# A trunk kernel's first mixer: modulation steps moved behind the gating, weight splits moved to VectorE, two engines put in written order

## The chip, the cores and the metric

The kernel runs on one core of a Trainium2 chip. The metric is the device time of one execution in microseconds (us); smaller is better. The engines are named as in the profile: PE (TensorE, matrix products), PEld (its weight loads), DVE (VectorE), ACT (ScalarE), POOL (GpSimd) and SP (SyncE, which here only issues DMA transfers). Each engine runs its own list of instructions in a fixed order and waits at the head of that list.

## The reference, cut to what matters

Two trunk layers, each a mixer and a gated feed-forward block, for 128 context tokens and 512 latent tokens. The change is all in the mixer of layer 0:

```python
sh1, sc1, g1, sh2, sc2, g2 = split(silu(c) @ w_mod[0] + b_mod[0], 6)   # for each of two streams
h = x * (1 + sc1) + sh1
z = h @ w_in
u = gelu(z[..., :512]);  v = gelu(z[..., 512:1024]);  p = z[..., 1024:]
vn = (v - mean(v)) * rsqrt(var(v) + eps)
s = einsum('hpq,bnqhc->bnphc', w_s, vn) + b_s         # spatial gate, chunks of 128 tokens
y_a = u * s
y_b = (pool_windows_2_4_8_16(p) - p) @ w_pool * pool_scale
x = layernorm(ALPHA * x + g1 * (concat(y_a, y_b) @ w_out))
```

`sh2`, `sc2` and `g1` (with `g2`, from later loads) are the modulation vectors not needed for `h`, but for what follows the mixer's output product.

## The kernel before, in words

All matrix products of this part are made in three passes of reduced-precision numbers: each operand is split into a high part (a cast) and a low part (operand minus high part), and line 152 multiplies high by high, line 153 high by low, line 154 low by high. A weight of 128x1024 is loaded into one of 4 buffers (tiles `r`), cast by ACT at line 99, and subtracted at line 102 by POOL or DVE into a pair of the 12 buffers `w`. `want` lists the weights in order with the engine for the subtraction, `load` starts a transfer, `prep` does the split, `take` hands out the next pair.

The first part (`even_first`) goes over eight slices e of the model width. For each slice `mod(e)` forms the slice's shift and scale on PE from 1 MB of weights (L717), ACT copies the result out (L720), `turn(e)` transposes it on PE (L726) and makes `h` on ACT and DVE (L728 to L737), and `product(e, 0..3)` adds the slice into four results in PSUM (L749 to L751): two output blocks of `u` and two token blocks of `v`. `warm` puts transposes of a unit matrix on PE. In the kernel before only PE's order is the written one in this part (`manual_schedule`); ACT, DVE and POOL are ordered by the scheduler, which builds each engine's list from priorities.

The second part (`even_mixer`) computes the three other token blocks of `v`, normalizes them (L812, L813, L158, L159 for the statistics, L818 for the scaling), and the `u` blocks 2 and 3, each of which is a pass of 48 products on PE into one of two PSUM tiles `A`. Then come four gatings (L871 on PE, five token blocks each; L874, L875, L878 on DVE) and four pooling passes p0 to p3. A pooling pass is again 48 products; ACT copies it out (L887, L888), DVE sums windows (L897 to L908), and `pool_out` multiplies by `w_pool` (six products). After that `out_proj` multiplies by `w_eo`.

Beside this runs the modulation that is needed later, as generators in the list `back`. Each `tick()` advances the first generator by one step. The first of them (`mod_vec`, L241 to L252) computes `sh2` on DVE: eight steps, each with two multiply-and-sum instructions of 128x1024 (L247). The second (`mod_pe`) computes `g1` and `sc2` on PE: eight steps, each with two 512 KB transfers (L281) and two bursts of small products (L292); after the last of them ACT copies the sums out (L298), PE transposes them (L302), DVE copies and adds (L306, L252), and `rows_out` transposes the result (L215) and writes it to memory (L217, L219), first for `g1`, then for `sc2`. `drain()` runs what is left of the generators, and `out_proj` follows.

Of the kernel before, what the change touches and what calls it, by code (L numbers as in the profile page):

```python
# [19 lines left out]
D = 1024  # L20
# [21 lines left out]
def tile_hybrid_trunk(ctx, tc, xT, x, vecs, tabs, wm0, wm1, wmT, crow, grow, lnrow, bs, w_u, w_v, w_p, w_s, w_pool, w_eo,  # L42
# [4 lines left out]
    dve, act, pe, pool, sp = nc.vector, nc.scalar, nc.tensor, nc.gpsimd, nc.sync  # L47
# [19 lines left out]
    def S(shape, dt=F32):  # L67
        return spool.tile(shape, dt, tag="s", name=nm("s"))

    def W(shape, dt=F32):  # L70
        return wpool.tile(shape, dt, tag="w", name=nm("w"))
# [22 lines left out]
    def f(ap):  # L94
        return ap.bitcast(F32)
# [16 lines left out]
    def want(src, shape, scale=None, lo=None):  # L112
        queue.append((src, shape, scale, lo))

    def load():
        src, shape, scale, lo = queue.pop(0)
        raw = R(shape)
        sp.dma_start(raw, src)
        loaded.append((raw, shape, scale, lo))

    def prep(lo_eng=None, pin=False):
        if not loaded:
            load()
        raw, shape, scale, lo_ = loaded.pop(0)
        lo_eng = lo_eng or lo_
        if scale is not None:
            dve.tensor_scalar(raw, raw, scale, ATTN_SCALE, ALU.mult, ALU.mult)
        hi, lo = W(shape, F32R), W(shape, F32R)
        with tc.high_priority() if urgent[0] else ExitStack():
            i = split(hi, lo, raw, act, lo_eng or pool)  # L130
        if pin:
            tc.keep_in_program_order(i)
        ready.append((hi, lo))
# [9 lines left out]
    def take():  # L143
        if not ready:
            prep()
        u = ready.pop(0)
        return u
# [17 lines left out]
    def tick(n=1):  # L165
        for _ in range(n):
            while back:
                try:
                    next(back[0])
                    break  # L170
                except StopIteration:
                    back.pop(0)
# [500 lines left out]
    def even_first(cb):  # L673
        want(w_u[0], [128, D])
        want(w_u[1], [128, D])
        want(w_v[0], [128, 2, 512])
        for k in range(1, 4):
            want(w_v[k], [128, 2, 512])
        for n in range(2, 4):
            want(w_u[n], [128, D], None, dve if n == 2 else None)  # L680
        for n in range(4):
            want(w_p[n], [128, D], None, dve if n % 2 == 0 else None)
        for k in range(8):
            want(w_eo[k], [128, D], None, dve if k >= 4 else None)

        xs = []
        wj = []

        def load_w(e):
            ts_ = [S([128, 4, 256]) for _ in range(2)]  # L690
            for q in range(2):
                sp.dma_start(ts_[q], wm0[e, q])
            wj.append(ts_)

        def load_x(e):
            t = Y([128, T])
            sp.dma_start(t, xT[e])
            xs.append(t)

        load_w(0)  # L700
        load_x(0)
        sp.dma_start(vec, vecs)
        load(), load(), load()
        b0 = cpool.tile([128, 8, 2], F32, name="b0")
        dve.tensor_copy(b0, vec[:, V_B0:V_B0 + 16].rearrange("p (e b) -> p e b", b=2))
        dve.tensor_scalar(b0[:, :, 1], b0[:, :, 1], 1.0, None, ALU.add)
        m0 = cpool.tile([128, 8, 2, 2], F32, name="m0")
        h = new_h()
        pad_h(h)
        psu = [A(), A()]  # L710
        psv = [B(), B()]

        def mod(e):
            ps = B()
            for k in range(8):
                g = k % 4
                pe.matmul(ps[32 * g:32 * g + 32, :256], sc32[:, k, :], wj[e][k // 4][:, k % 4, :],  # L717
                          start=k < 4, stop=k >= 4, tile_position=(0, 32 * g))
            r = Tm([128, 256])
            act.copy(r, ps[:, :256])  # L720
            return r

        def turn(e, r):
            pt = B()
            for b in range(2):
                pe.transpose(pt[:, b * 128:(b + 1) * 128], r[:, b * 128:(b + 1) * 128], ident)  # L726
            p4 = pt[:, :256].rearrange("p (b g s) -> p s b g", b=2, s=32)
            dve.tensor_reduce(m0[:, e], p4[:, 0:2], AX.X, ALU.add)  # L728
            dve.tensor_tensor(m0[:, e], m0[:, e], b0[:, e:e + 1, :].to_broadcast([128, 2, 2]), ALU.add)
            hi, lo = hk(h, e, slice(0, T))  # L730
            t = Tm([128, T])
            for s, (a, b) in enumerate(((0, 128), (LAT0, T))):
                sh, sc = m0[:, e, s, 0:1], m0[:, e, s, 1:2]
                act.activation(hi[:, a:b], xs[e][:, a:b], AF.Identity, bias=sh, scale=sc)
                dve.tensor_scalar(t[:, a:b], xs[e][:, a:b], sc, sh, ALU.mult, ALU.add)
            for (a, b) in ((0, 128), (LAT0, T)):
                dve.tensor_tensor(lo[:, a:b], t[:, a:b], f(hi[:, a:b]), ALU.subtract)  # L737

        def product(k, n):
            if n < 2:  # L740
                w = (us[n][0][:, k * 128:(k + 1) * 128], us[n][1][:, k * 128:(k + 1) * 128])
                for (s, m, c) in G:
                    part(psu[n][:, c:c + m], w, hk(h, k, slice(s, s + m)), k)
            else:
                w = (vu[k // 2][0][:, k % 2, :], vu[k // 2][1][:, k % 2, :])
                part(psv[n - 2], hk(h, k, slice(TOK[n - 2], TOK[n - 2] + 128)), w, k)

        def part(out, a, b, k):
            pe.matmul(out, a[0], b[0], start=k == 0, stop=False)  # L749
            pe.matmul(out, a[0], b[1], start=False, stop=False)  # L750
            pe.matmul(out, a[1], b[0], start=False, stop=k == 7)  # L751

        for e in range(1, 5):
            load_w(e)
            load_x(e)
            if e % 2 == 0:
                load()

        def warm(n):
            for _ in range(n):  # L760
                pe.transpose(psv[0][:, 0:128], ident, ident)

        vu, us = [], []
        with tc.manual_schedule(engines={mybir.EngineType.PE}):
            warm(16)
            r = mod(0)
            warm(3)
            turn(0, r)
            for e in (dve, pool, dve):
                prep(e)  # L770
            us.extend([take(), take()])
            vu.append(take())
            warm(8)
            r = mod(1)
            for e in range(8):
                product(e, 0)
                if e < 7:
                    turn(e + 1, r)
                product(e, 1)
                product(e, 2)  # L780
                if e < 6:
                    r = mod(e + 2)
                    if e + 5 < 8:
                        load_w(e + 5)
                        load_x(e + 5)
                        if e == 1:
                            load()
                product(e, 3)
                if e in (0, 2, 4):
                    prep()  # L790
                    vu.append(take())
        sp.dma_start(tab, tabs)
        for s in range(2):
            sp.dma_start(cb[s], crow[s:s + 1].to_broadcast([128, D]))
        load()
        return h, vu, psu, psv

    def even_mixer(make_norm, nxt_sub):
        cb = [V([128, D]) for _ in range(2)]
        h, vu, psu, psv = even_first(cb)  # L800
# [31 lines left out]
        for i in range(2, 5):  # L832
            c = slice(TOK[i], TOK[i] + 128)
            ps = B()
            mm3(ps, [(*hk(h, k, c), vu[k // 2][0][:, k % 2, :], vu[k // 2][1][:, k % 2, :]) for k in range(8)])
            v_scale(i - 2)
            if i == 2:
                bsb = S([128, 4, 128])
                sp.dma_start(bsb, bs.to_broadcast([128, 512]))
                wst = S([128, 4, 128])  # L840
                sp.dma_start(wst, w_s)
                wp_raw = R([128, 4, 128])
                sp.dma_start(wp_raw, w_pool)
            tick(2)
            v_stats(i, ps)
        v_scale(3)
        for n in range(2, 4):
            u = take()
            hold[0] = 3
            pump()  # L850
            ps = A()
            ntile(u, h, ps)
            u_out(n, ps)
            if n == 2:
                v_scale(4)
            else:
                wp = (W([128, 4, 128], F32R), W([128, 4, 128], F32R))
                split(wp[0], wp[1], wp_raw, act, pool)
            tick(2)
        back.append(mod_pe(0, (2, 4)))  # L860
        tick()
        ycat = ([None] * 4, [None] * 4)
# [689 lines left out]
```

## Time and profile before

| | |
|---|---|
| median of 3 runs | 1537.13 us (1536.52 to 1538.94) |
| the profiled execution | 1539.92 us |
| its span | 1538.10 us |
| PE busy | 1470.3 us, 96% |
| PEld busy | 1324.0 us, 86% |
| DVE busy | 993.5 us, 65% |
| ACT busy | 597.4 us, 39% |
| POOL busy | 569.8 us, 37% |
| PE in the chain that ended last | 31% of the span |

The span is cut into 40 slices on the page; the first four, some 154 us, hold all that the change touches. PE is busy 7, 9, 8 and 9 tenths there, against 9 in nearly all the others. The mean granted clock of PE over the execution is 0.977 of full speed.

### The profile page before, as it was taken

The page shows a single profiled execution, that of the slowest core. Times are in us where ns is not written, and L with a number is a line of the kernel's source. Part 1 is how long each engine was busy: PE and PEld are TensorE (multiplying, and loading weights), DVE is VectorE, ACT ScalarE, POOL GpSimd, SP SyncE. Part 2 cuts the span into 40 slices and gives each one's busy share as a digit, 9 for nine tenths or more (in the row PEclk, how much of TensorE's full clock was granted, in tenths as well). Part 3 has the DMA queues.
Part 4 walks back from the last instruction along what each step waited for, and adds up shares of the span by engine and source line. Part 5 has one row for each costly group of instructions (what it writes and reads, how often), then busy time and mean ns, then how long its engine had stood idle before and what let it go on. Part 6 is the DMA issues. An engine that isn't in the chain of part 4 may idle for free. (4 is left out here: it accounts for less than half of the span.)

```text
span 1538.1 us, 21978 instructions
## 1 busy us (share of the span) xinstructions
PE 1470.3 (96%) x8768; PEld 1324.0 (86%) x8768; DVE 993.5 (65%) x1491; ACT 597.4 (39%) x889; POOL 569.8 (37%) x445
## 2 busy tenths in 40 slices
PE   7989999999999999999979999998999999999997
PEld 5866879989898989888968788787998989898995
DVE  4775687547867797677789577767854424333557
ACT  3422354333141323235755566526433323232323
POOL 2231444333242524543476301764423232142343
PEclk9989999999999999999989899999999999999998
DMA  9544706235443544333011002351533313133231
GB/s 377 215 163 155 273 33 199 97 124 178 153 167 130 168 164 155 113 144 108 26 65 52 7 1 86 121 191 35 199 101 119 114 61 96 34 110 110 69 110 69
DMA packets 54757, 188.10 MB, mean 122 GB/s; under 512 B 6592, under 2 KB 7168, under 8 KB 54656
## 3 DMA queue, kind: packets, MB, share of 16 engines
q1 hardware_dynamic: 54656, 186.71, 35.8%
q8 instruction: 69, 1.13, 0.3%
q14 instruction: 32, 0.26, 0.1%
HBM read 175.96 MB, written 10.72 MB: 121 GB/s over the span
## 5 line engine op out<-in xcount | busy, mean ns | idle before, releaser
L102 POOL TENSOR_TENSOR w<-r,w 128x1024 fp32r<-128x1024 f32 (+3 forms) x136 | 339.9, 2509 | 681.6 <-ACT w L99 681.3
L152 PE MATMUL A<-s,w 128*128 128x258 f32 (+1 forms) x1672 | 525.6, 315 | 11.7 <-DVE t L556 4.5
L153 PE MATMUL A<-s,w 128*128 128x258 f32 (+1 forms) x1672 | 523.3, 313 | 0.5 <-DVE s L102 0.5
L154 PE MATMUL A<-s,w 128*128 128x258 f32 (+1 forms) x1672 | 522.3, 313 | 1.1 <-POOL w L102 1.1
L152 PEld LDWEIGHTS A<-s,w 128*128 128x128 f32 x1672 | 319.1, 191 | 23.0 <-issue 13.3
L153 PEld LDWEIGHTS A<-s,w 128*128 128x128 f32 x1672 | 319.4, 191 | 4.2 <-issue 2.5
L154 PEld LDWEIGHTS A<-s,w 128*128 128x128 f32 x1672 | 319.6, 191 | 3.9 <-issue 2.5
L99 ACT CAST w<-r 128x1024 fp32r<-128x1024 f32 (+3 forms) x184 | 186.1, 1029 | 343.4 <-PE B L153 137.4
L153 PE MATMUL B<-w,s 128*128 128x512 f32 (+2 forms) x734 | 284.2, 387 | 6.0 <-DVE w L102 6.0
L152 PE MATMUL B<-w,s 128*128 128x512 f32 (+2 forms) x734 | 284.5, 389 | 4.1 <-DVE y L492 2.9
L154 PE MATMUL B<-w,s 128*128 128x512 f32 (+2 forms) x734 | 283.1, 387 | 1.0 <-DVE s L102 1.0
L555 DVE SCALAR_TENSOR_TENSOR t<-A,vec,t 128x641 f32<-128x641 f32 x88 | 77.7, 883 | 218.5 <-ACT t L554 218.5
L153 PEld LDWEIGHTS B<-w,s 128*128 128x128 f32 x734 | 139.9, 191 | 33.8 <-DVE w L102 7.1
L152 PEld LDWEIGHTS B<-w,s 128*128 128x128 f32 x734 | 140.1, 191 | 32.3 <-DVE y L492 3.5
L154 PEld LDWEIGHTS B<-w,s 128*128 128x128 f32 x734 | 139.9, 191 | 29.3 <-DVE s L102 1.4
L247 DVE SCALAR_TENSOR_TENSOR t<-r,v 128x1024 bf16<-128x1024 f32 x112 | 157.6, 1417 | 4.6 <-DMA r<-in_wmT_dram 3.5
L99 ACT CAST s<-t 128x642 fp32r<-128x642 f32 x60 | 43.8, 730 | 182.2 <-DVE t L566 147.7
L102 DVE TENSOR_TENSOR w<-r,w 128x1024 fp32r<-128x1024 f32 (+3 forms) x48 | 71.8, 1512 | 60.9 <-ACT w L99 60.8
L492 DVE TENSOR_TENSOR y<-B,y 128x512 f32<-128x512 f32 x80 | 54.8, 688 | 61.7 <-PE B L154 61.7
L554 ACT ACTIVATE t<-A,vec 128x642 f32<-128x642 f32 x88 | 77.8, 884 | 16.6 <-PE A L154 16.6
L556 DVE SCALAR_TENSOR_TENSOR t<-A,vec,t 128x641 f32<-128x641 f32 x88 | 77.8, 884 | 2.5
L102 DVE TENSOR_TENSOR s<-t,s 128x642 fp32r<-128x642 f32 x60 | 55.5, 925 | 25.6 <-ACT s L99 25.5
(257 smaller groups left out, 1614.9 us busy)
## 6 DMA issues: line engine op xcount, KB each, us to landing
r<-in_w_up_dram SPq DMA_DIRECT2D x88, 512.0 KB, 3.7
r<-in_wmT_dram SPq DMA_DIRECT2D x56, 512.0 KB, 3.4
r<-in_w_dn_dram SPq DMA_DIRECT2D x44, 512.0 KB, 4.0
s<-scr SPq DMA_DIRECT2D x20, 512.0 KB, 7.9
s<-in_wm_dram SPq DMA_DIRECT2D x16, 512.0 KB, 9.2
r<-in_wm_dram SPq DMA_DIRECT2D x16, 512.0 KB, 4.6
kept<-y SPq DMA_DIRECT2D x10, 512.0 KB, 3.9
r<-kept SPq DMA_DIRECT2D x10, 512.0 KB, 3.5
```

Source lines behind the costliest of these rows:

```text
L99: act.copy(hi, src)
L102: return lo_eng.tensor_tensor(lo, src, f(hi), ALU.subtract)
L152: pe.matmul(out, ah, bh, start=i == 0, stop=False)
L153: pe.matmul(out, ah, bl, start=False, stop=False)
L154: pe.matmul(out, al, bh, start=False, stop=i == n - 1)
L247: op = dve.scalar_tensor_tensor(junk, raw, 1.0, cb[s], ALU.mult, ALU.mult, accum_out=mc[l][:, m, s, k:k + 1])
L492: dve.tensor_tensor(acc[i][:, sl], ps, acc[i][:, sl], ALU.add)
L554: act.activation(t, z, AF.Identity, bias=cb, scale=w1)
L555: dve.scalar_tensor_tensor(t[:, 1:], z[:, :T - 1], w0, t[:, 1:], ALU.mult, ALU.add)
L556: dve.scalar_tensor_tensor(t[:, :T - 1], z[:, 1:], w2, t[:, :T - 1], ALU.mult, ALU.add)
```

## The change

1. In the first part ACT and DVE too now follow the written order.
2. The three first weights are all split on DVE (before: DVE, POOL, DVE), after `turn(0)` in the order of both engines. The three other `v` weights are split on DVE (before: POOL), at slices 1, 3 and 5, between `product(e, 1)` and `product(e, 2)` (before: after `product(e, 3)` of slices 0, 2 and 4).
3. The four pooling weights `w_p` are split on DVE (before: two on DVE, two on POOL).
4. Two calls of `tick(2)` in the second part, in loops of three and two passes, become `tick()`: five modulation steps fewer ahead of the gating. The generators are the same, so the steps come later.

```diff
@@ even_first
         for n in range(4):
-            want(w_p[n], [128, D], None, dve if n % 2 == 0 else None)
+            want(w_p[n], [128, D], None, dve)
...
-        with tc.manual_schedule(engines={mybir.EngineType.PE}):
+        with tc.manual_schedule(engines={mybir.EngineType.PE, mybir.EngineType.Activation, mybir.EngineType.DVE}):
...
-            for e in (dve, pool, dve):
-                prep(e)
+            for _ in range(3):
+                prep(dve)
...
                 product(e, 1)
+                if e in (1, 3, 5):
+                    prep(dve)
+                    vu.append(take())
                 product(e, 2)
...
                 product(e, 3)
-                if e in (0, 2, 4):
-                    prep()
-                    vu.append(take())
@@ even_mixer
-            tick(2)
+            tick()
             v_stats(i, ps)
...
-            tick(2)
+            tick()
         back.append(mod_pe(0, (2, 4)))
```

The rows below are the engines' lists in their fixed order. Names are tiles with a running number, which differs between the two kernels.

DVE around the first two gatings, before. L818 scales the last two token blocks of `v`, L247 are modulation steps, L874 and L875 take the first gating out of PSUM tile `A_917`:

```order
L102 TENSOR_TENSOR w_851<-r_787,w_850 128x1024
L813 BN_AGGR m_768<-m_767 128x2
L818 TENSOR_SCALAR s_602<-s_602,m_724,m_727 128x512
L818 TENSOR_SCALAR s_603<-s_603,m_768,m_771 128x512
L247 SCALAR_TENSOR_TENSOR t_844,mc_107<-s_761,v_125 128x1024
L247 SCALAR_TENSOR_TENSOR t_847,mc_107<-s_842,v_125 128x1024
L247 SCALAR_TENSOR_TENSOR t_844,mc_107<-s_761,v_126 128x1024
L247 SCALAR_TENSOR_TENSOR t_847,mc_107<-s_842,v_126 128x1024
L252 TENSOR_TENSOR mc_107<-mc_107,vec 128x16
L874 TENSOR_TENSOR t_923<-A_917,s_662 128x128
L875 TENSOR_TENSOR t_923<-A_917,s_662 128x512
L878 TENSOR_TENSOR t_923<-t_923,s_604 128x642
```

The same place after; the first gating's tile is `A_904`:

```order
L818 TENSOR_SCALAR s_602<-s_602,m_714,m_717 128x512
L818 TENSOR_SCALAR s_603<-s_603,m_753,m_756 128x512
L247 SCALAR_TENSOR_TENSOR t_829,mc_107<-s_746,v_126 128x1024
L102 TENSOR_TENSOR w_931<-r_774,w_930 128x1024
L247 SCALAR_TENSOR_TENSOR t_894,mc_107<-s_827,v_125 128x1024
L247 SCALAR_TENSOR_TENSOR t_894,mc_107<-s_827,v_126 128x1024
L247 SCALAR_TENSOR_TENSOR t_899,mc_107<-s_892,v_125 128x1024
L874 TENSOR_TENSOR t_910<-A_904,s_662 128x128
L247 SCALAR_TENSOR_TENSOR t_899,mc_107<-s_892,v_126 128x1024
L875 TENSOR_TENSOR t_910<-A_904,s_662 128x512
L874 TENSOR_TENSOR t_923<-A_917,s_662 128x128
L878 TENSOR_TENSOR t_910<-t_910,s_604 128x642
```

Fewer modulation steps stand ahead of the gating in all, and none of the last stand as a block before L874; one of them now stands between L874 and L875 of the first gating.

DVE on the way from the fourth gating (tile `A_1006`) to the first pooled result `s_1037`, after; before, no L247 stood on this way:

```order
L875 TENSOR_TENSOR t_1012<-A_1006,s_662 128x512
L102 TENSOR_TENSOR s_992<-t_999,s_991 128x642
L878 TENSOR_TENSOR t_1012<-t_1012,s_605 128x642
L102 TENSOR_TENSOR s_992<-t_1012,s_991 128x642
L247 SCALAR_TENSOR_TENSOR t_1024,mc_107<-s_1019,v_125 128x1024
L897 TENSOR_TENSOR t_1027<-t_985 128x671
L247 SCALAR_TENSOR_TENSOR t_1024,mc_107<-s_1019,v_126 128x1024
L904 TENSOR_TENSOR t_1027<-t_1027,tab 128x8 x4
L252 TENSOR_TENSOR mc_107<-mc_107,vec 128x16
L907 SCALAR_TENSOR_TENSOR t_1033<-t_1027,t_985 128x128
L908 SCALAR_TENSOR_TENSOR t_1033<-t_1027,t_985 128x512
```

The last modulation step of `mod_vec` now stands in the middle of the first pooling.

PE at the end of the pooling, before. `A_1358` is the third `pool_out`, `B_1444` the first tile of `out_proj`; the transposes L302 stand 44 rows earlier:

```order
L153 MATMUL A_1358<-s_1292,w_906 128x384
L154 MATMUL A_1358<-s_1292,w_907 128x384
L215 MATMUL B_1367<-ident,m_1276 16x128
L215 MATMUL B_1401<-ident,m_1379 32x128
L152 MATMUL B_1444<-w_1070,s_915 128x512
```

The same place after:

```order
L292 MATMUL B_1117<-r_1272,sc_98 32x512 x2
L154 MATMUL A_1343<-s_1265,w_889 128x384
L292 MATMUL B_1117<-r_1273,sc_98 32x512 x2
L302 MATMUL B_1354<-ident,t_1352 128x128 x4
L215 MATMUL B_1386<-ident,m_1365 16x128
L215 MATMUL B_1401<-ident,m_1398 32x128
L152 MATMUL B_1444<-w_1041,s_902 128x512
```

The last bursts L292 and the transposes L302 moved from the middle of p3 to the very end: between the last burst and `out_proj` PE has only L302 and the two L215.

## Rows read from the trace of the kernel before

**Rows 1.** Table by stretch: us, length, PE busy (instructions), granted clock, DMA share, GB/s.

```profile
89.60:99.80 10.20, 6.11 (x30) 0.50 0.18 65
121.00:136.10 15.10, 15.10 (x82) 1.00 0.81 272
...
216.00:218.00 2.00, 2.00 (x11) 0.50 0.00 0
```

**Rows 2.** Instructions of PE in time: start, length, line, shapes, [idle before, releaser].

```profile
77.50 0.28 PE L152 MATMUL A<-s,w 128*128 128x258 f32 x1
...
84.61 1.05 PE L871 MATMUL A<-s,s 128*128 128x128 f32 x8
87.72 0.49 PE L871 MATMUL A<-s,s 128*128 128x128 f32 x2 [2.06 <-DVE s L818]
...
95.41 0.55 PE L152 MATMUL A<-s,w 128*128 128x258 f32 x1 [4.09 <-DVE t L875]
...
104.47 1.28 PE L871 MATMUL A<-s,s 128*128 128x128 f32 x10
...
106.67 1.38 PE L871 MATMUL A<-s,s 128*128 128x128 f32 x10
...
108.96 0.39 PE L152 MATMUL A<-s,w 128*128 128x258 f32 x1
...
215.75 1.12 PE L431 MATMUL B<-ident,t 128*128 128x128 f32 x4 [2.39 <-DVE t L417]
```

**Rows 3.** The same view, DVE and POOL around the gating.

```profile
84.81 2.34 POOL L102 TENSOR_TENSOR w<-r,w 128x1024 fp32r<-128x1024 f32 x1
...
84.88 2.79 DVE L818 TENSOR_SCALAR s<-s,m,m 128x512 f32<-128x512 f32 x1 [0.71 <-POOL m L159]
87.59 1.21 DVE L247 SCALAR_TENSOR_TENSOR t<-s,v 128x1024 bf16<-128x1024 f32 x1
...
94.58 0.68 DVE L875 TENSOR_TENSOR t<-A,s 128x512 f32<-128x512 f32 x1
...
122.76 2.45 DVE L904 TENSOR_TENSOR t<-t,tab 128x8 f32<-128x8 f32 x4
```

**Rows 4.** The same view, ACT around the first gating.

```profile
85.61 1.04 ACT L99 CAST w<-r 128x1024 fp32r<-128x1024 f32 x1 [2.83 <-DMA r<-in_w_eo_dram]
86.57 0.70 ACT L821 ACTIVATE s<-A 128x642 f32<-128x642 f32 x1
```

**Rows 5.** The same view, the first part: PE, then DVE.

```profile
15.70 1.93 PE L717 MATMUL B<-s,sc 128*32 128x256 f32 x16
...
17.56 0.49 PE L749 MATMUL A<-s,w 128*128 128x258 f32 x1
...
23.27 0.38 PE L726 MATMUL B<-ident,t 128*128 128x128 f32 x2
...
28.41 0.38 PE L726 MATMUL B<-ident,t 128*128 128x128 f32 x2
...
33.00 0.38 PE L726 MATMUL B<-ident,t 128*128 128x128 f32 x2
...
23.89 1.62 DVE L729 TENSOR_TENSOR m<-m,b 128x4 f32<-128x4 f32 x1
```

**Rows 6.** DMA issues of the page: tile, count, KB each, median us from issue to landing.

```profile
r<-in_wm_dram SPq DMA_DIRECT2D x16, 512.0 KB, 4.6
```

**Rows 7.** Instructions in time at the end of the pooling: ACT, PE, DVE.

```profile
140.06 0.59 ACT L298 COPY t<-B 128x512 f32<-128x512 f32 x1 [2.03 <-PE B L292]
...
140.72 0.65 PE L302 MATMUL B<-ident,t 128*128 128x128 f32 x4
...
148.81 0.38 PE L215 MATMUL B<-ident,m 128*16 128x128 f32 x2
...
148.06 1.23 DVE L102 TENSOR_TENSOR w<-r,w 128x1024 fp32r<-128x1024 f32 x1 [0.17 <-ACT w L99]
...
150.76 2.62 DVE L897 TENSOR_TENSOR t<-t 128x669 f32<-128x669 f32 x3
```

## The prediction

> **What bounds the kernel now.** I read the page first: PE is busy 96% of the span, so time can only come from stretches where PE idles or runs at the lower clock. Of the part that the change touches, the slices put the first (the start, loads) and the third (77 to 115 us) below 9 tenths. The table by stretch shows it at half clock: 0.50 from 89.6 to 99.8 [rows 1], the 1.2 GHz level. PE's instructions in time then give the cause [rows 2]. The `u` pass 3 begins at 77.50 and ends at 84.61, so a pass of 48 products costs 7.1 us. The first gating starts at 84.61, stops before its last token block, waits 2.06 us for the scaling L818 and goes on at 87.72. The pooling pass p0 waits another 4.09 us for L875 and begins at 95.41; begun at half clock, it lasts until 104.47, 9.1 us instead of 7.1. From 84.61 to 104.47 are 19.9 us for work of some 10. Last I asked VectorE and GpSimd [rows 3]: L818 took 2.79 us at 84.88, because a GpSimd split started at 84.81 and held it off until 87.15; then four L247 of 1.2 us each (87.59 the first) stood ahead of L875 of 94.58. So the wait that ends last is VectorE's list: modulation steps ahead of the gating.
>
> **The change part by part.** Times are against the profiled execution, 1539.92 us, which is 2.79 above the median; I add the sum to the median.
>
> *Gating.* Five of eight modulation steps ahead of it go (two L247 each, 12 us of VectorE); four splits of 1.2 us come to VectorE there. L818 is then done about 8 us before PE is through with the `u` passes, and the 2.06 us vanish. What is late next: the second gating needs ScalarE's L821, which still follows a cast that waits for the weight buffer that `u` pass 3 frees; 1.04 and 0.70 us [rows 4] put the second gating 1.9 us after the first, an idle of 0.65. Then p0 needs L875, and the order puts an L247 between L874 and L875. That L247 becomes ready about 1.5 us after the end of pass 3; the GpSimd split behind the same cast starts at 1.1 and lasts 2.34 [rows 3]. If it holds VectorE off as it did L818, L247 ends at 4.7, L875 (0.68) at 5.4, p0 starts at 5.5 instead of 10.8. The idle before it is 2.4 us, and after an idle of 2.39 us elsewhere [rows 2] the clock of the next stretch was 0.50 [rows 1], so I add 1.5 for p0's clock (9.1 less 7.1 is the upper bound, 0 the lower). Stretch: 5.5 + 7.1 + 1.5 = 14.1 against 19.9, **-5.8**. Bounds: p0 at 3.4 with full clock, -9.4; p0 at 5.5 with all the loss of before, -5.3.
>
> *First part.* PE began its products at 17.56, after `mod(1)` of 15.70 at half clock [rows 5]. After, ScalarE copies the first result out before its three casts of 1.04 each instead of behind them, so PE arrives at `mod(1)` some 5 us earlier and waits for that slice's weights. When they land, no row shows: between the two arrivals, since `mod(1)` did not wait at 15.70. DMA is 9 tenths busy in the page's first slice, so I take a value in the later half, 13.5; two us of `mod(1)` put the products at 15.6, and half of the gain is given back at half clock: **-1.0** (0 to -3; 0 if they land just as PE came before). Later slices: the transposes L726 come 5.1 us apart at one and 4.6 at the next (23.27, 28.41, 33.00), because at every second slice a GpSimd split held VectorE's L729 for 1.62 us [rows 5]. No GpSimd split is left there; the VectorE split that replaces it fits behind `turn`, where VectorE waits for the next transposes. Three times 0.55: **-1.7** (-1.0 to -1.7). The split of the first weights on VectorE instead of GpSimd, and that of `w_p`, cost nothing: PE is busy with `mod(1)` and the `u` passes meanwhile; uncovered it would be 1.2 each.
>
> *Gatings 3 and 4.* Before, 4.5 us from 104.47 to 108.96 [rows 2], which held two bursts of `mod_pe`. Those are now later: 2.2 us between the two gatings' starts (104.47, 106.67), set by ScalarE's copy of p0, plus 1.3: 3.5, so -1.0. In return fourteen bursts instead of twelve follow p1. One costs 1.2: the fully busy 15.1 us from 121.0 [rows 1] hold a pass (7.1), a `pool_out` of six products (0.9) and six bursts. 2 x 1.2 - 1.0 = **+1.4**. The transfers of `mod_pe` wait on SyncE behind the last modulation load, whose buffer the fourth gating frees; with 4.6 us to landing [rows 6] against 7 us of p1, the first arrive in time, and from then on bursts are as far apart as before: 0 (up to +3).
>
> *First `pool_out`.* It now stands right behind p1 and one burst. Its input comes through VectorE: from the end of the third gating's products some 12 us of L874 to L908, with two L247 in the middle and one hold by the GpSimd split that p0's buffer releases. That makes the input ready 1.5 us after PE asks. A second hold is possible: p1's buffer releases the next GpSimd split just when L904 is due, and before, at such a place, L904 took 2.45 us [rows 3]; then it is 4.0. The two start within 0.1 us of each other, so I take the middle, 2.8, and 1.7 for the clock after it: **+4.5** (1.5 to 5.9).
>
> *End of pooling.* After the last burst PE has nothing but L302 and the two L215, and `out_proj` stands behind them. Before, the same chain ran under p3. The steps: L298 0.59, L302 0.65 [rows 7], three VectorE copies and an addition 0.7, first L215; then VectorE has a split of 1.23 and three L897 of 0.87 between the small additions for `sc2`, 4.6 us with them, and only then the second L215. PE is idle 0.65 + 0.75 + 4.6 = 6.0; the clock is down when `out_proj` starts, for which I take the 1.5 of p0 again: **+7.5** (6.0 with full clock, 8.0 with the 2.0 that p0 lost before). The gate `g1` is no later than that: its load follows the second L215 by 5 us, and PE fills its four PSUM tiles for 11.
>
> Sum: -5.8 - 1.0 - 1.7 + 1.4 + 4.5 + 7.5 = **+4.9 us**, 1537.1 + 4.9 = **1542.0**.
>
> **The rivals.**
> (A) *No hold at the two places.* If L247 gets ahead of the GpSimd split at the first gating and L904 ahead of it at the first pooling, p0 starts 2.1 us earlier at full clock (-9.4) and `pool_out` waits 1.5 at full clock. 4.9 - 3.6 - 3.0 = -1.7: 1535.4, not slower. It decides at L247: either it starts before 1.1 us after pass 3, or the cast comes later than that. Before, the cast came 1.0 us after the end of pass 3, not at once [rows 4]; but there it waited for its transfer, and that one is now asked for 7 us earlier. The Trainium skill (SBUF — State Buffer, section Who interferes with whom) says that of a VectorE instruction with two inputs in SBUF and a GpSimd one that reads it, the first to be issued blocks the other for its whole length. The trace agrees (L818, 2.79 us), so order of arrival alone would make A.
> (B) *A, and the clock stays up at the end of pooling.* Another -1.5: 1533.9, faster. Against it: every idle of over 2 us that I looked at was followed by 0.50.
> (C) *The bursts wait for their transfers.* Fourteen bursts in 32 us where before twelve took 40; a wait of about 1 us at three of them, with clock, is +4: 1546.
> (D) *The gating comes no earlier.* The Trainium skill (Perfetto Trace Analysis, section Optimizing Scalar/DVE Operations) warns that moving work between VectorE and GpSimd might not help, since they share a port. Were the splits moved to VectorE to delay L818 as much as the steps did, the 5.8 would go: 1547.8. Four splits against ten L247 speak against it.
>
> **How the numbers follow.** Forecast 0.50; A 0.26, B 0.12, C 0.09, D 0.03. A measurement of this kernel tells 0.2%, 3.1 us, from no change. Slower: forecast, C and D, 0.62. Same: A, 0.26. Faster: B, 0.12. The range leaves out D, part of B and the upper ends: 1534.5 to 1546.5.
>
> **What would show it.** Right: PE's products begin before 16.5 us; transposes L726 are 4.6 apart throughout; L818 for the last block is done before the first gating starts; p0 is released by L875, which an L247 of over 2 us preceded; L152 of the first `pool_out` waits for ScalarE's cast 1.5 to 4 us; and ahead of `out_proj` PE idles 6 us in three pieces, the last released by L210 on VectorE, with clock 0.50 after it. Wrong: `out_proj` starting before 147 us (before, it starts just behind the L215 of 148.81 [rows 7]), or PE busy between the last burst and `out_proj`.

## The result, and the profile after

| | before | after |
|---|---|---|
| median | 1536.83 us (1535.56 to 1538.94, 4 runs) | 1550.07 us (1549.05 to 1551.68, 4 runs) |
| ratio | | 1.0082 (95% interval 1.0070 to 1.0094) |
| the profiled execution, its span | 1539.92, 1538.10 us | 1549.50, 1547.70 us |
| mean granted clock of it | 0.977 | 0.975 |

The change makes the kernel 13.2 us slower by the medians, 9.6 between the two profiled spans. By the ratio it is 12.6 us. 4.9 us were forecast; the sign was right, the size was not, and 1550.1 lies above the range. A second comparison (after_again, below) gave 1.0071 (1.0051 to 1.0091), 10.9 us.

PE's share of the span on the page, 95% (before 96%), hides this; PE in time around the places of the prediction shows it (start, length, line, shapes, [idle before, releaser]):

```profile
81.56 1.27 PE L871 MATMUL A<-s,s 128*128 128x128 f32 x10
83.34 1.38 PE L871 MATMUL A<-s,s 128*128 128x128 f32 x10 [0.50 <-ACT s L821]
...
86.95 0.55 PE L152 MATMUL A<-s,w 128*128 128x258 f32 x1 [2.23 <-DVE t L875]
...
96.67 1.28 PE L871 MATMUL A<-s,s 128*128 128x128 f32 x10
98.49 1.38 PE L871 MATMUL A<-s,s 128*128 128x128 f32 x10 [0.54 <-ACT t L888]
99.63 0.37 PE L152 MATMUL A<-s,w 128*128 128x258 f32 x1
...
112.18 0.50 PE L152 MATMUL A<-s,w 128*128 128x258 f32 x2 [3.00 <-ACT s L99]
...
147.27 0.66 PE L302 MATMUL B<-ident,t 128*128 128x128 f32 x4 [0.69 <-ACT t L298]
148.68 0.28 PE L215 MATMUL B<-ident,m 128*16 128x128 f32 x1 [0.75 <-DVE m L210]
153.03 0.40 PE L215 MATMUL B<-ident,m 128*32 128x128 f32 x1 [4.07 <-DVE m L210]
153.08 0.78 PE L152 MATMUL B<-w,s 128*128 128x512 f32 x1
...
221.77 0.66 PE L431 MATMUL B<-ident,t 128*128 128x128 f32 x4 [2.37 <-DVE t L417]
```

These rows answer [rows 2, 7]. The waits of 2.06 for L818 and 4.09 for L875 are gone; in their place stand 2.23 for L875, 3.00 at the first `pool_out` (112.18) and 0.69, 0.75 and 4.07 in front of `out_proj`, which begins at 153.08. In before it begins at

```profile
148.94 0.48 PE L152 MATMUL B<-w,s 128*128 128x512 f32 x1
```

The L431 of 221.77 is a good mark for all that follows: in every kernel PE waits there 2.4 us for L417, at the end of layer 0's mixer. In before it is at 215.75 [rows 2], so after is 6.02 us behind when the changed stretch and its clock are through. From there on both kernels run the same instructions in the same order, and still after loses 3.6 us more between these two executions, with a granted clock of 0.98 in both (stretches 260 to 1530 and 266 to 1540).

The first part, PE, answers [rows 5]:

```profile
12.99 1.08 PE L717 MATMUL B<-s,sc 128*32 128x256 f32 x8 [4.07 <-DMA s<-in_wm_dram]
14.26 1.08 PE L717 MATMUL B<-s,sc 128*32 128x256 f32 x8 [0.20 <-DMA s<-in_wm_dram]
15.28 0.58 PE L749 MATMUL A<-s,w 128*128 128x258 f32 x1
...
17.05 0.63 PE L726 MATMUL B<-ident,t 128*128 128x128 f32 x2
...
21.94 0.38 PE L726 MATMUL B<-ident,t 128*128 128x128 f32 x2
```

The products begin at 15.28 (before 17.56). VectorE and GpSimd at the first gating, and VectorE at the first pooling, answer [rows 3]:

```profile
82.76 2.35 POOL L102 TENSOR_TENSOR w<-r,w 128x1024 fp32r<-128x1024 f32 x1 [1.98 <-ACT w L99]
...
83.09 3.10 DVE L247 SCALAR_TENSOR_TENSOR t<-s,v 128x1024 bf16<-128x1024 f32 x1
86.12 0.68 DVE L875 TENSOR_TENSOR t<-A,s 128x512 f32<-128x512 f32 x1
...
104.81 1.22 DVE L247 SCALAR_TENSOR_TENSOR t<-s,v 128x1024 bf16<-128x1024 f32 x1
...
106.73 1.22 DVE L247 SCALAR_TENSOR_TENSOR t<-s,v 128x1024 bf16<-128x1024 f32 x1
...
107.87 2.55 DVE L904 TENSOR_TENSOR t<-t,tab 128x8 f32<-128x8 f32 x4
...
108.02 2.38 POOL L102 TENSOR_TENSOR w<-r,w 128x1024 fp32r<-128x1024 f32 x1 [5.24 <-PE B L292]
```

Both holds that the forecast took are there: the GpSimd split came 0.33 us ahead of L247, which then took 3.10 us instead of 1.22; and L904, late behind two moved L247, was caught by the split of 108.02 and took 2.55. The Trainium skill (SBUF — State Buffer, section Who interferes with whom) says that the first of the two to be issued blocks the other; the trace agrees. The rule as the prediction cites it is one of VectorE instructions with two inputs in SBUF; L247 is such a one, where L818, the prediction's example, has one tensor and two columns of scalars.

### The profile page after: what moved, and what is told of

It is laid out like the page before. It is cut to its first block, busy times and chain, and to the rows that moved or that the text cites. A ratio compares the mean times of both kernels' runs of the same rounds, so it can differ in the third digit from the quotient of the medians.

```text
span 1547.7 us, 21967 instructions
## 1 busy us (share of the span) xinstructions
PE 1474.1 (95%) x8768; PEld 1327.2 (86%) x8768; DVE 991.4 (64%) x1497; ACT 597.8 (39%) x889; POOL 553.0 (36%) x439
## 5 line engine op out<-in xcount | busy, mean ns | idle before, releaser
L102 POOL TENSOR_TENSOR w<-r,w 128x1024 fp32r<-128x1024 f32 (+3 forms) x130 | 323.9, 2502 | 664.5 <-ACT w L99 642.2
L152 PEld LDWEIGHTS A<-s,w 128*128 128x128 f32 x1672 | 318.6, 191 | 23.8 <-issue 12.9
L99 ACT CAST w<-r 128x1024 fp32r<-128x1024 f32 (+3 forms) x184 | 185.8, 1028 | 351.7 <-PE B L153 138.8
L247 DVE SCALAR_TENSOR_TENSOR t<-r,v 128x1024 bf16<-128x1024 f32 x112 | 156.5, 1407 | 4.5 <-DMA r<-in_wmT_dram 3.6
L102 DVE TENSOR_TENSOR w<-r,w 128x1024 fp32r<-128x1024 f32 (+3 forms) x54 | 79.7, 1493 | 60.2 <-ACT w L99 60.2
L99 ACT CAST s<-t 128x642 fp32r<-128x642 f32 x60 | 43.8, 730 | 174.3 <-DVE t L566 147.5
L554 ACT ACTIVATE t<-A,vec 128x642 f32<-128x642 f32 x88 | 77.7, 883 | 14.9 <-PE A L154 14.9
L102 DVE TENSOR_TENSOR s<-t,s 128x642 fp32r<-128x642 f32 x60 | 57.0, 949 | 25.3 <-ACT s L99 25.2
```

Of the source, the lines that this page charges most:

```text
L99: act.copy(hi, src)
L102: return lo_eng.tensor_tensor(lo, src, f(hi), ALU.subtract)
L152: pe.matmul(out, ah, bh, start=i == 0, stop=False)
L247: op = dve.scalar_tensor_tensor(junk, raw, 1.0, cb[s], ALU.mult, ALU.mult, accum_out=mc[l][:, m, s, k:k + 1])
L554: act.activation(t, z, AF.Identity, bias=cb, scale=w1)
```

## The experiments

Three questions: which part of the change costs the time; whether the two waits cost what the forecast said; and what makes the unchanged code behind `out_proj` slower. "Mark" is the L431 above; each ratio is against before on the same chip.

| kernel | mark, us | against 215.75 | 48 products in layer 0, layer 1, us | ratio (95% interval) |
|---|---|---|---|---|
| after | 221.77 | +6.0 | 7.167, 7.120 | 1.0082 (1.0070 to 1.0094) |
| after_again | 218.03 | +2.3 | 7.167, 7.120 | 1.0071 (1.0051 to 1.0091) |
| ticks_only | 223.57 | +7.8 | 7.169, 7.120 | 1.0099 (1.0078 to 1.0119) |
| no_ticks | 214.37 | -1.4 | 7.121, 7.074 | 0.9997 (0.9985 to 1.0009) |
| late_finish | 213.02 | -2.7 | 7.167, 7.120 | 1.0042 (1.0027 to 1.0057) |
| one_back | 218.98 | +3.2 | 7.114, 7.073 | 1.0041 (1.0026 to 1.0056) |
| tick_first | 215.15 | -0.6 | 7.122, 7.074 | 1.0032 (1.0016 to 1.0047) |
| late_first | 207.91 | -7.8 | 7.121, 7.074 | 0.9970 (0.9957 to 0.9982) |
| shift | 218.10 | +2.4 | 7.108, 7.093 | 1.0032 (1.0018 to 1.0046) |
| place_a | 212.48 | -3.3 | 7.120, 7.073 | 1.0009 (0.9998 to 1.0019) |
| place_b | 214.03 | -1.7 | 7.167, 7.120 | 1.0031 (1.0018 to 1.0044) |
| late_place_own | 208.38 | -7.4 | 7.167, 7.120 | 1.0009 (0.9994 to 1.0023) |
| late_place | 208.70 | -7.0 | 7.123, 7.073 | 0.9988 (0.9979 to 0.9997) |

The fourth column is the median spacing of L554 (it follows each pass of 48 products) in stretches where PE never idles; before has 7.120 and 7.074.

### Which part

ticks_only is before with the two `tick(2)` made `tick()`.

> The kernel before, with the two calls tick(2) made tick() and nothing else. Theory T (the loss is the moved modulation steps): after stands 6.0 us behind before from 160 to 340 us of the span, of which the first part gave -3.0; so without the first part's edits the steps alone make +9.0 there, and PE again waits for VectorE's L210 (some 4 us) and for L99 ahead of the first pool_out (some 3 us): 1537 + 9 = 1546, more with whatever the later code adds. Rival F (the first part's written order or the w_p splits on VectorE cost the time, not the steps): these two waits are not there or are short, and the time is within 3 us of before, 1534 to 1540.

no_ticks is after with both put back.

> The changed kernel with both tick(2) put back: the first part's edits and the w_p splits on VectorE alone. Theory T: the first part's gain of 3.0 us (as in the trace of after at 60 us) stays, the two waits at the end of the pooling and at the first pool_out are gone, and the gating waits as before or 1 us less (four splits of 1.2 us have come to VectorE in place of GpSimd, which held it): 1537 - 3 = 1534, between 1531 and 1537. Rival F: 1546 or more.

Theory T holds. The steps alone cost as much as the whole change, 1.0099 (the intervals overlap), and their mark is 7.8 behind; the first part and the splits on VectorE alone are no change that can be told, 0.9997. Their mark is 1.4 us ahead instead of 3.0: in this execution PE waited 5.69 us for the weights of `mod(1)` and began it at 14.22 (after: 12.99), so that the first gating starts 1.44 ahead of before, and nothing is won or lost behind it up to the mark. Part of what the steps cost is no wait at all: in the fourth column ticks_only has after's values and no_ticks before's, which the third question takes up.

### The waits that the moved steps leave

late_finish takes the second L215 out of the way of `out_proj`:

```diff
-        drain()
+        while not g1_out: tick()
         gate = mod_bc(0, SG1)
...
-        yield from rows_out(l, [(SG1, mc[l][:, 2])])
+        yield from rows_out(l, [(SG1, mc[l][:, 2])]); g1_out.append(1)
         yield from finish_b(l)
```

> The changed kernel, but ahead of out_proj the generators are run only until g1 has been written out; the end of finish_b (the second L215 and its two stores) goes behind the second output tile of out_proj. Theory T: the wait of 4.07 us for L210 goes and with it the part of the half clock that follows (151.4 to 158.2 in after, some 2 to 3 us); the two short waits of 0.7 us stay: 5.5 to 7 us less than after, 1543 to 1544.5. Rival (the wait only hides another one, since the input of out_proj or its gate g1 is no earlier): less than 2 us of gain, 1548 to 1550.

In front of `out_proj` PE now has, in time:

```profile
144.95 0.66 PE L302 MATMUL B<-ident,t 128*128 128x128 f32 x4 [0.69 <-ACT t L298]
146.36 0.28 PE L215 MATMUL B<-ident,m 128*16 128x128 f32 x1 [0.75 <-DVE m L210]
146.39 0.48 PE L152 MATMUL B<-w,s 128*128 128x512 f32 x1
```

The 4.07 are gone and nothing takes their place. Behind them the clock is up, where after had 0.66:

```profile
150.00:160.00 10.00, 10.00 (x47) 8.22 (x46) 5.84 (x16) 3.91 (x5) 1.68 (x2) 1.00 0.90 324
```

The ratio falls from 1.0082 and 1.0071 to 1.0042, 4.5 to 6.1 us, where 5.5 to 7 were expected.

one_back puts one step back ahead of the gating (`tick()` behind `back.append(mod_pe(...))` becomes `tick(2)`), so that no L247 stands in the first pooling.

> The changed kernel with one modulation step put back ahead of the gating (the tick() behind mod_pe is tick(2)), so that no L247 stands between the third gating and the first pooled result. Theory T (the first pool_out waits since two L247 of 1.2 us and their holds stand on VectorE's way there): its wait of 3.0 us for ScalarE's cast falls to under 1.5, worth 1.5 to 3 us, and up to 2 us more of clock; p0 and the end of the pooling as in after; 2 to 5 us less than after where the tiles s lie alike (they lie in a third way here: 44 passes of layer 1 keep six of eight tiles of before, so 1 to 3 us less again). Rival (the wait comes from elsewhere on that path, the hold by GpSimd at L904): still 2.5 us or more.

The wait for L99 at the first `pool_out` is not there at all: PE's rows go from one instruction to the next. On VectorE no L247 stands on the way to L904, and the hold is gone too:

```profile
105.55 0.39 DVE L904 TENSOR_TENSOR t<-t,tab 128x8 f32<-128x8 f32 x4
```

So the wait came from the moved step; how much of it was the two L247 and how much the hold that they brought L904 into, this run doesn't separate. But the mark is only 2.8 us ahead of after, and 1.0 behind after_again, since one wait became longer, that of p0:

```profile
88.88 0.55 PE L152 MATMUL A<-s,w 128*128 128x258 f32 x1 [3.70 <-DVE t L875]
```

tick_first is after with `tick(2)` in the first of the two loops again (three of five steps back); late_first is tick_first and late_finish together.

> The changed kernel with the first of its two loops at tick(2) again: three of the five moved steps back ahead of the gating, two behind it; the end of finish_b stands in front of out_proj as in after. The tiles s lie as in before (one pass 7.120 and 7.074 us). It splits late_first (0.9970) into its two edits. Theory T (the price of the moved steps is the wait they leave at the end): with three steps fewer behind the gating, L302 and the first L215 stand among p3's and pool_out's products, and only the second L215 waits, for what is left of its 4.1 us: time 1534 to 1539, 1 to 4 us more than late_first. Rival (the three steps alone bring the gain, nothing is left to wait for): as late_first, 0.9957 to 0.9982 of before.

> late_finish with the first of the two loops at tick(2) again: three of the five moved steps are back ahead of the gating, two stay behind it, and the end of finish_b goes into out_proj. The tiles s of the later code then lie as in before. Theory: L818 of the last block was done some 8 us before its gating in after, so three steps of 2.4 us fit there; the gating keeps its gain, no L247 stands in the first pooling, L302 and the first L215 come under p3 again: the first part's -3.0 to -1.4, the gating's -4 to -5, bursts +0.5 to +1.4: 5 us less than before, 1532 (1529 to 1535). Rival (three steps are too many: L875 of the first gating waits for four L247 again, as in before): 1536 or more.

The two differ in the wait for the second L215 and what hangs on it. PE in time, tick_first:

```profile
142.71 0.33 PE L154 MATMUL A<-s,w 128*128 128x384 f32 x1
146.74 0.40 PE L215 MATMUL B<-ident,m 128*32 128x128 f32 x1 [3.69 <-DVE m L210]
146.79 0.77 PE L152 MATMUL B<-w,s 128*128 128x512 f32 x1
```

and by stretch (us, length, each engine's busy time, granted clock, DMA share, GB/s), tick_first, then late_first:

```profile
138.00:148.00 10.00, 4.01 (x18) 2.80 (x17) 9.25 (x31) 3.54 (x8) 0.10 (x1) 0.78 0.01 2
148.00:158.00 10.00, 10.00 (x39) 8.01 (x39) 2.90 (x4) 2.84 (x4) 1.43 (x2) 0.88 0.88 317
```

```profile
138.00:148.00 10.00, 9.15 (x45) 7.16 (x44) 9.30 (x32) 3.35 (x7) 0.10 (x1) 1.00 0.41 120
148.00:158.00 10.00, 10.00 (x47) 8.30 (x46) 4.89 (x7) 7.33 (x9) 5.12 (x5) 1.00 1.00 402
```

At the mark late_first is 7.24 us ahead: 3.69 of idle, 1.45 of two shorter waits just ahead of it (for L99 0.84 against 0.37, for L102 0.98 against none), and some 2 of products at half clock. By the ratios it is 0.0062, 9.5 us, uncertain by some 3; the executions' mean granted clock is 0.977 in tick_first and 0.981 in late_first. I expected 1 to 4: a wait of 3.7 us here costs about twice its own length, or more. late_first is the version that beats both kernels: 1533.83 against 1538.46 us, 0.9970, 4.6 us. It keeps the early gating (p0 starts at 90.79, in before at 95.41) and has neither new wait.

### What makes the unchanged code slower

shift is before with `warm(8)` as `warm(32)`.

> The kernel before with 24 more warm-up transposes on PE in front of mod(1), nothing else: at some 0.23 us each by the rows of the start (eight took 1.92 us), every later product starts about 5.5 us later, as it does in after from 160 us on (+6.0). It asks why after lost 13.2 us by the medians (9.6 between the two profiled spans), when the two traces are 6.0 apart at 340 us and run the same code in the same order from there. Theory S (that code takes more or less time when it starts at another time, since its waits and the clock fall differently): the end is later than the offset at 260 us by something other than 0, up to 7 us; time 1543 to 1550. Rival N (the rest is something the change leaves behind in the later code, its buffers or its order): the end is 5.5 us later, 1542.3 within 1.5.

The mark moves by 2.35, not by 5.5 (32 transposes took 5.34 us, less than the rows of the start had let expect, and `mod(1)` then ran in 1.07 instead of 1.93), and the ratio gives 4.9. That is 2.6 more, but the two theories' numbers were made for another offset, and shift has values of its own in the fourth column: it decides nothing. What it showed is that this column takes only a few values, the same to 0.003 us in kernels that are otherwise unlike. The eight tiles `s` that hold `h` (high and low part of each quarter, in the order in which a pass reads them) lie in these of the 18 buffers `s`, each 5152 bytes of a partition, and the kernels with the same list have the same two times:

```
                                       layer 0                layer 1
before no_ticks tick_first late_first  9 5 13 17 6 2 8 3      6 4 9 15 2 7 14 12
after ticks_only late_finish           9 17 13 7 5 3 6 1      5 8 9 15 3 0 14 12
shift                                  9 4 13 17 5 2 8 6      5 3 9 15 2 7 14 12
one_back                               9 7 13 1 6 3 2 17      6 4 9 15 3 8 14 12
```

The pool hands out whichever buffer comes free, and the last modulation loads (`s` too) now take and return theirs at other times, so that from there on all later tiles lie elsewhere. place_a and place_b test this alone. In both, every tile gets its buffer from a table:

```diff
-    spool = ctx.enter_context(tc.tile_pool(name="spool", bufs=18))
+    spool = ctx.enter_context(tc.tile_pool(name="spool", bufs=1))
...
-        return spool.tile(shape, dt, tag="s", name=nm("s"))
+        return spool.tile(shape, dt, tag=f"s{next(slot)}", name=nm("s"))
```

> The kernel before with its 18 buffers s named one by one: each of its 236 tiles s is put by a table into the buffer that it has in before, so every address is that of before (some orders change, since the scheduler now sees 18 buffers in place of one pool). It is the partner of place_b, which has the same instructions in the same order with the same waits. It is made because the same 48 products take 7.120 us in layer 0's feed-forward block and 7.074 in layer 1's in the traces of before and no_ticks, 7.167 and 7.120 in after, ticks_only and late_finish, and because those two groups are also the two ways in which the tiles s lie in SBUF. Theory P (the address of the tiles that PE reads sets this): passes of 7.120 and 7.074. Rival Q (it comes from something else in the program): any value, but the same as in place_b.

> place_a with its table renamed one to one, so that the tiles s lie as they do in after; instructions, order and waits are those of place_a, only addresses differ. Theory P: passes of 7.167 and 7.120 us, output tiles of twelve 512-column products of 2.793 and 2.827 in place of 2.783 and 2.767, and the whole later than place_a by 88 passes x 0.047 = 4.1, 220 triples x 0.0025 = 0.6 and 220 x 0.015 = 3.3: 8 us (5 to 10). Rival Q: the time of place_a within 2 us.

ACT in time, place_a, then place_b; L554 follows each pass:

```profile
1269.73 0.89 ACT L554 ACTIVATE t<-A,vec 128x642 f32<-128x642 f32 x1
...
1276.81 0.89 ACT L554 ACTIVATE t<-A,vec 128x642 f32<-128x642 f32 x1
...
1283.88 0.89 ACT L554 ACTIVATE t<-A,vec 128x642 f32<-128x642 f32 x1
```

```profile
1281.36 0.88 ACT L554 ACTIVATE t<-A,vec 128x642 f32<-128x642 f32 x1
...
1288.48 0.88 ACT L554 ACTIVATE t<-A,vec 128x642 f32<-128x642 f32 x1
...
1295.60 0.88 ACT L554 ACTIVATE t<-A,vec 128x642 f32<-128x642 f32 x1
```

Passes are 7.07 to 7.08 apart and 7.12, with the same instructions, order and waits and PE busy without a break (30.00 of 30 us in both). late_finish was made into the same kind of pair:

> late_finish (the changed kernel with the end of finish_b moved into out_proj) with its buffers s named one by one, at its own addresses, which are those of after. Partner of late_place. Theory P: passes of 7.167 and 7.120; the time is that of late_finish, 1543, as far as the scheduler's other order in the changed stretch leaves it (1539 to 1549). Rival Q: passes as in late_place.

> late_place_own with the table renamed so that the tiles s of the later code lie as in before; instructions, order and waits the same. Theory P: passes of 7.120 and 7.074 and 8 us less than late_place_own (5 to 10), which would put it ahead of before if late_place_own is no slower than late_finish: 1535. Rival Q: the time of late_place_own within 2 us.

The passes came out as expected in all four. The whole did by sign: 1.0031 to 1.0009 is 3.4 us, 1.0009 to 0.9988 is 3.2 us. The intervals of each pair still touch, and each size is uncertain by some 2.6 us. The mean granted clocks in a pair are alike (0.980 and 0.981, 0.983 and 0.982). late_place_own lies as late_finish does and is at 1.0009 instead of 1.0042; in its other order no wait is left ahead of p0, and 0.73 us instead of 2.93 at the first `pool_out`.

That is less than the 8 expected: the passes give 88 x 0.047 = 4.1, but the 0.06 per output tile that I had put on all of layer 1 holds only for one block of ten tiles, and most others differ by less than 0.02, some with the other sign.

The traces give the size more closely. Take the products behind the mark that stand at full clock and without idle in both of two traces, and sum the differences of the time from one start to the next: place_b needs 4.1 us more than place_a and late_place_own 4.5 more than late_place. Against before, after needs 4.3, after_again 4.5 and ticks_only 4.6 more; no_ticks and late_first, which have before's list, need 0.0 and 0.1 more. Theory P is shown for the tiles `s` as a whole, all of which move in a pair; which of them count, and why an address costs time, is not.

### Once more

> The changed kernel once more, beside the two that follow, for its median over more executions and a second profile. The placement of the tiles s cost 3 to 4 us in two pairs (place_b against place_a 1.0031 to 1.0009, late_place_own against late_place 1.0009 to 0.9988), and the changed stretch 6.0 in the first profile: 9 to 10 us together. If these two are all, the median is 1537.5 + 9.5 = 1547 and the ratio 1.006; if a third loss exists in the later code, 1550 again (1.0082), with a granted clock below 0.977.

The ratio lies between the two that were named. The executions went from 1542.33 us at a mean granted clock of 0.982 to 1551.34 at 0.974, and the profiled one is the first of these. It waits just as long as the profile of after (2.22 for L875, 3.06 for L99, 0.69, 0.75 and 4.07 at the end), but its mark is 3.7 earlier. By stretch, after, then after_again:

```profile
80.00:90.00 10.00, 7.28 (x44) 6.92 (x44) 8.89 (x14) 2.38 (x3) 2.45 (x2) 0.80 0.11 44
90.00:100.00 10.00, 9.46 (x59) 9.27 (x58) 4.75 (x8) 2.42 (x4) 2.13 (x1) 0.86 0.00 0
110.00:120.00 10.00, 7.82 (x39) 4.60 (x41) 6.54 (x15) 2.14 (x3) 0.62 (x5) 0.83 0.57 193
150.00:160.00 10.00, 6.97 (x22) 5.57 (x23) 5.29 (x17) 1.24 (x3) 0.00 (x0) 0.66 0.45 137
```

```profile
80.00:90.00 10.00, 7.28 (x55) 6.92 (x55) 8.88 (x15) 2.38 (x3) 2.45 (x2) 1.00 0.07 29
90.00:100.00 10.00, 9.46 (x69) 9.27 (x68) 7.31 (x11) 3.16 (x5) 2.59 (x5) 1.00 0.29 92
```

The same idle ahead of p0 brings the clock down in one execution and leaves it at full speed in the other; p0 takes 9.72 us in the first (86.95 to 96.67) and 7.16 in the second. A forecast of one value for the clock behind such a wait is a mean over both.

## Why the prediction was right or wrong

Step by step, in the profile of after, against [rows 2, 5, 7]:

| step | forecast | measured |
|---|---|---|
| first part (start and odd slices), at the first gating | -2.7 | -3.05 (81.56 against 84.61) |
| gating, to the end of p0 | -5.8 | -4.75 (15.11 us against 19.86); -7.3 in after_again |
| gatings 3 and 4 | -1.0 | -1.53 (2.96 against 4.49) |
| p1 to `out_proj`: two bursts, `pool_out`, three waits | +2.4 +4.5 +6.0 = +12.9 | +13.47 (53.45 against 39.98) |
| clock behind the start of `out_proj` | +1.5 | +1.88 (6.02 at the mark, 4.14 at `out_proj`) |
| sum at the mark | +4.9 | +6.02; +2.28 in after_again |
| everything behind | 0 | +3.6 between the two profiled spans |

**Right:** the mechanism, item for item. Products before 16.5 us (15.28); p0 released by L875 behind an L247 of over 2 us (3.10); ScalarE's cast late by 1.5 to 4 at the first `pool_out` (3.00); three pieces of idle ahead of `out_proj`, 5.5 us where 6.0 were said, the last released by L210, and `out_proj` at 153.08, not before 147. L818 for the last block was done before the first gating, though 5.6 us before the end of the `u` passes and not 8. Transposes L726 are 4.6 apart from the second on (the first pair, 17.05 and 21.94, at partly half clock, is 4.9). C's waits for transfers are 0.16 and 0.51 us, inside the bounds. A, B and D didn't come: both holds were there in both profiles of after, and the gating came earlier.

**Wrong, the step that failed:** "1537.1 + 4.9". Everything behind the stretch was taken at nothing, without a word, because its code and order are unchanged. Its addresses are not. The placement of the tiles `s` costs 3.3 us by two pairs of kernels, 4.1 to 4.6 by the products themselves. A sum of the local terms couldn't hold it, and the range went 9.4 us above the median, which beside the 6.0 at the mark left 3.4. That the two profiled executions lie 3.6 apart there is near this size by luck: 4.3 more in products at full clock, 2.6 less in products at half clock, 1.9 more around idle. after_again needs 4.5 more in the first, 4.7 less in the second, and comes out 0.1 behind before.

**Wrong, the size of a term:** the clock. Gating took 1.5 us for p0's clock with 2.0 as upper bound; p0 took 2.6 more than a pass in the first profile and nothing more in the second. Rival B's counter-argument, that every idle of over 2 us is followed by 0.50, fell with after_again. And the end of the pooling was sized right in this trace (5.5 of idle, 1.9 of clock), but to take its longest wait away is worth 4.5 to 6.1 us by the ratios from after to late_finish and 9.5 from tick_first to late_first. Besides, the terms were taken against an execution at a mean clock of 0.977 and added to the median of executions that run at 0.980.

**What stays open:** The profiled spans are 9.6 us apart, where the two comparisons say 12.6 and 10.9 by their ratios. Part of the rest comes from which executions were profiled: their mean clocks are 0.977 in before and 0.975 in after, while the 98 executions of before in the four later comparisons average 0.980 and the ten of after and after_again 0.976. Over those 98 the time falls by 1.05 us for each 0.001 of clock, so by this estimate after loses another 1.6 us, 11.2 in all. The clock does fall more in after; behind which of its waits, over many executions, two profiles of it can't tell. And it wasn't found which addresses are fast.

## What to carry to other kernels

Moving work that takes buffers from a shared pool can move the address of every later tile; compare the time of one unchanged, fully busy pass far behind the change before blaming the change's own waits, and let a forecast carry a few us of either sign for it. Steps that fill one engine ahead of a wait are best moved only as far as the slack goes: two of the five were enough here, and a short chain that nothing needs yet (the second L215) belongs behind the next long product, not in front of it. Count an idle of 2 to 4 us on PE at its own length at least and at up to two and a half times that, as the pairs here show, and expect executions to differ by it.

## What the runs showed of the hardware

- 48 products that PE runs without a break take 7.074, 7.093 or 7.120 us in layer 1 and 7.108 to 7.167 in layer 0, according to the SBUF buffers that the tiles `s` lie in, alike to some 0.003 us in all kernels with the same list, on different executions; place_a and place_b differ in nothing else.
- The same wait of 2.2 us went with a granted clock of 0.80 and 0.86 in the two stretches of 10 us around it in one execution, and of 1.00 in both in another. The Trainium skill (TensorE: Matmul & The Clock Gate, Part 1) says of the start of a kernel that the time at the lower clock varies from run to run; this pair shows it in the middle of one.
- An execution follows its clock: those of after_again go from 1542.33 us at 0.982 to 1551.34 at 0.974, more than most of the changes studied here. Over 98 executions of before it is 1.05 us for each 0.001 of mean granted clock.
